# A hybrid block on one core: the plain slab of the second product stored in two parts, and the state space's outer products moved to GpSimd

## The chip, the cores and the metric

One core of a Trainium2 chip runs the whole block. The metric is device microseconds of one execution; lower is better.

## The reference, cut to what matters

`x` is 1024 positions by 1024 channels, all float32. `u`, `val`, `cg`, `bg`, `gs`, `gc` are column blocks of one input projection.

```python
xn = rmsnorm(x);  proj = xn @ w_in + b_in
y  = s5_branch(u)            # 32 groups of 16 channels, 64 complex states each, a linear scan over the positions
ya = (gelu(y) @ w_glu_a) * sigmoid(gelu(y) @ w_glu_b)
yb = (bg * conv3(cg * val)) @ w_conv_out
h  = x + (sigmoid(gs) * ya + sigmoid(gc) * yb) @ w_out
h  = h + square(relu(rmsnorm(h) @ w_ff1)) @ w_ff2      # 1024 -> 4096 -> 1024
return rmsnorm(h)
```

## The kernel before, in words

Activations lie transposed, channels on the 128 partitions and positions along the free dimension. A float32 operand is cut into a rounded high part and the rest, its low part (a Copy on ScalarE, a subtraction on VectorE), and one product of a 128x128 block is three matmuls of 512 columns: high by high, high by low, low by high. Every engine runs its instructions in the order in which the program issues them; no scheduler reorders them. Tiles come from rings of slots: `apool` (34 slots of 128x1024, tag "u"), `wpool` (6), `tpool` (6 slots of 128x512, `half`).

**The state space beside the projections.** `order` (line 146) lists 57 jobs on TensorE. The state space runs beside them as generators: `ssm_step(s)`, s = 0 to 7, two state groups each. `products` (line 131) adds to a credit account `BESIDE[job]` times 0.648 for each product and calls `draw` after every fourth; `draw` resumes the generators as long as the account is over zero, and each `yield` of a positive number is taken from it. A `yield` of a negative number lets the generator rest for so much of the planner's PE time. So the numbers in the `yield`s decide behind which product each piece of a step stands in every engine's order. A step computes two outer products (`outer`, line 473: a table `Bk` and a table `Vk`, each from two multiplications and two half-height subtractions or additions for the real and for the imaginary part), then phases on VectorE (`f`, `k`, `a1`), two Sin on ScalarE, four transposes of `Bk` (`pst`, line 523) and eight small matmuls of `Vk` by `Bk` (`psk`, line 526) on TensorE, a copy `WT` on ScalarE, the input matmuls (`psxr`, `psxi`, line 539), the scan on VectorE and the output matmuls (`psy`). Step s + 1 is started when the input matmuls of step s are issued. Before step 0, `ssm_params` computes the tables `dsc`, `asc`, `bbr`, `bbi`, `th`, `tl` on GpSimd.

**The feed-forward layer.** Its first product is done in 14 groups (`seven`, line 1204) of seven chains of 12 matmuls (P1 to P7 of a fast two-by-two scheme), with the callbacks `after(0)` to `after(6)` between them: P1, `after(0)`, P4 of the group before, `after(1)`, P5, `after(2)`, P2, `after(3)`, P6, `after(4)`, P3, `after(5)`, P7, `after(6)`. P4 adds into the bank `seed`, which `done(g, "c22")` reads on VectorE after P7 (line 1283). The last group has no group behind it, so its P4 follows its P7 at once. Results go to memory through GpSimd's DMA queue: groups 2 to 13 in the arrangement that the second product wants (the sums `t1` and `n2` already cut in a high and a low part, `split_out`, line 1256; the low part is made at the next `after`), groups 0 and 1 and the four plain blocks as whole rows `h2d`. The second product starts with a plain slab: the rows 24 to 27, which groups 0 and 1 wrote. `slab_load` (line 1160) fetches them at `after(0)` of the last group, and `slab_cut` (line 1166) cuts each into high and low in `after(3)` to `after(6)` of that group; `w2_cut(24)` fetches and cuts the first weight at `after(4)`. Then come 16 plain products (`pf`, line 1350), 12 groups of seven chains with the weights prepared by the lists `SECOND` (line 1075), and the last slab.

Of the kernel before, what the change touches and what calls it, by code (L numbers as in the profile page):

```python
# [9 lines left out]
F32 = mybir.dt.float32  # L10
F32R = mybir.dt.float32r
I32 = mybir.dt.int32
AF = mybir.ActivationFunctionType
ALU = mybir.AluOpType

P = 128
D = 1024
S = 1024
# [6 lines left out]
DFF = 4096  # L25
N_PLAIN = 4
N_GROUP = (32 - N_PLAIN) // 2
FIRST_PLAIN = 32 - N_PLAIN
N_CHUNK = 3
# [17 lines left out]
def block_kernel(ctx, tc, x_t, par, ssm, w_u, win, wco, wglu, wo, w1, w2, out):  # L47
    nc = tc.nc
    V, A, G, T = nc.vector, nc.scalar, nc.gpsimd, nc.tensor
# [8 lines left out]
    def unit(name, dt=F32):  # L58
        return apool.tile([P, S], dt, tag="u", name=name)

    def half(name, dt=F32):
        return tpool.tile([P, HALF], dt, tag="t", name=name)
# [4 lines left out]
    HS = [slice(0, HALF), slice(HALF, S)]  # L67
# [79 lines left out]
    for i in range(8):  # L147
        order.append(("val", i))
        if i in conv_out_after:
            r = conv_out_after[i]  # L150
# [26 lines left out]
    for k in range(8):  # L177
# [8 lines left out]
        t = unit(f"xr{k}")  # L186
# [272 lines left out]
    def sh(name):  # L459
        return swork.tile([P, HALF], F32, tag="sh", name=name)  # L460
# [4 lines left out]
    def ssm_step(s):  # L465

        q = slice(2 * s, 2 * s + 2)
# [5 lines left out]
        def outer(n, ar_, ai_, xr_, xi_, dst, first):  # L473
            w = 2 * n * 16
            ba = lambda z: z[:, q, :].unsqueeze(3).to_broadcast([P, 2, n, 16])
            bx = lambda z: z[:, q, :].unsqueeze(2).to_broadcast([P, 2, n, 16])
            for r in range(2):
                t = sh(f"o{s}_{n}_{r}")
                t1, t2 = (t[:, i * w:(i + 1) * w].rearrange("p (a l c) -> p a l c", a=2, l=n) for i in range(2))
                V.tensor_mul(t1, ba(ar_), bx(xi_ if r else xr_))  # L480
                V.tensor_mul(t2, ba(ai_), bx(xr_ if r else xi_))
                f = V.tensor_add if first == r else V.tensor_sub
                for g in range(2):
                    rows = slice(64 * g, 64 * g + 64)
                    f(dst[rows, :, r, :, g, :], t1[rows], t2[rows])

        outer(4, dsc_r, dsc_i, bbr, bbi, Bk.rearrange("p a r (j g c) -> p a r j g c", j=4, g=2), 1)
        yield 1.7
        outer(5, asc_r, asc_i, bc_raw[:, 2], bc_raw[:, 3], Vk.rearrange("p a r (l g c) -> p a r l g c", l=5, g=2), 0)
        yield 1.9  # L490


        th, tl = names["th"], names["tl"]
        f, k, a1 = sh(f"f{s}"), sh(f"k{s}"), sh(f"a{s}")
# [48 lines left out]
        xr, xi, t = sh(f"xr{s}"), sh(f"xi{s}"), sh(f"t{s}")  # L543
# [15 lines left out]
        yr, t2 = sh(f"yr{s}"), sh(f"t2{s}")  # L559
# [25 lines left out]
        if s % 2:  # L585
            for c in HS:
                y = U[s // 2].rearrange("p q c -> p (q c)")[:, c]
                t = sh(f"gz{s}_{c.start}")
# [65 lines left out]
    for k in range(8):  # L654
# [10 lines left out]
        for h in range(2):  # L665
            for e in range(3):
                wc = slice(o + e * P, o + (e + 1) * P)
                c = HS[h]
# [40 lines left out]
    h = [None] * 8  # L709
    wo_w = []  # L710
    dram = ctx.enter_context(tc.tile_pool(name="dram", bufs=1, space=bass.MemoryType.DRAM))
    hd = [dram.tile([P, S], F32, tag=f"hd{i}", name=f"hd{i}") for i in range(8)]
    h2d = {i: dram.tile([P, S], F32, tag=f"h2d{i}", name=f"h2d{i}") for i in range(8 * N_CHUNK, DFF // P)}
    xd = {
        (q, nm, part): dram.tile([P, 4, HALF], F32, tag=f"xd{q}{nm}{part}", name=f"xd{q}{nm}{part}")
        for q in range(N_CHUNK) for nm in X_OF.values() for part in ("hl" if nm in SPLIT else "r")
# [41 lines left out]
    for n in range(n_main):  # L758
        job = order[n]
        k, i = job[0], job[1]  # L760
# [49 lines left out]
        elif k == "val":  # L810
            cur["v"] = []
            for hh in range(2):
                t, t2 = half(f"v1_{n}_{hh}"), half(f"v2_{n}_{hh}")
# [3 lines left out]
        elif k == "cg":  # L817
            vp = spool.tile([P, S + 2], F32, tag="vp", name=f"vp{i}")
            V.memset(vp[:, 0:2], 0.0)
            for hh in range(2):  # L820
                t = half(f"c1_{n}_{hh}")
# [18 lines left out]
        elif k == "bg":  # L840
            vh, vl = unit(f"vh{i}", F32R), unit(f"vl{i}", F32R)
            for hh in range(2):
                t = half(f"b1_{n}_{hh}")
                t2 = half(f"b2_{n}_{hh}")
# [7 lines left out]
        elif k in ("gs", "gc"):  # L852
            if k == "gs":
                gs[i] = unit(f"gs{i}")
            for hh in range(2):
                t = half(f"g1_{n}_{hh}")
# [4 lines left out]
                else:  # L861
                    t2 = half(f"g2_{n}_{hh}")
                    A.activation(t2, t, AF.Sigmoid, bias=b)
                    V.tensor_mul(Y[i][:, HS[hh]], Y[i][:, HS[hh]], t2)
        elif k == "glu":
            mh, ml = unit(f"mh{i}", F32R), unit(f"ml{i}", F32R)
            for hh in range(2):
                pb, pa = ps[2 * hh], ps[2 * hh + 1]
                t, t2 = half(f"s1_{n}_{hh}"), half(f"s2_{n}_{hh}")
# [138 lines left out]
    def rows_of(g):  # L1008

        if g < 2:  # L1010
            return 8 * N_CHUNK + 2 * g, 8 * N_CHUNK + 2 * g + 1
        q, c = divmod(g - 2, 4)
        return 8 * q + c, 8 * q + 4 + c
# [53 lines left out]
    def steps_of(g, plan):  # L1067

        for step in plan:
            for what in step.split():  # L1070
                gw[g]["do"]["shl".index(what[0])](what[1])
            yield

    FIRST = ["", "", "s1 h0", "l0 h1", "l1"], ["s2 h2", "l2", "h3", "l3"]
    SECOND = ["", "", "", "s1 h3", "h1 l3", "l1"], ["s2 h0", "l0 h2", "l2"]

    def group_steps(g, own):

# [2 lines left out]
        if "do" not in gw[g]:  # L1081
            gw[g]["do"] = w_parts(g)
        return steps_of(g, (SECOND if g >= N_GROUP else FIRST)[own])

# [71 lines left out]
    slab = {}  # L1156
    raw2 = {}
    w2p = {}

    def slab_load(s):  # L1160
        for c in range(4):
            t = unit(f"fl{s}_{c}", F32R)
            nc.sync.dma_start(t.bitcast(F32), h2d[4 * s + c])
            raw2[s, c] = t

    def slab_cut(s, c):
        hi, lo = unit(f"fh{s}_{c}", F32R), raw2.pop((s, c))
        A.activation(hi, lo.bitcast(F32), AF.Copy)
        V.tensor_sub(lo, lo.bitcast(F32), hi.bitcast(F32))
        slab.setdefault(s, []).append((hi, lo))  # L1170
# [70 lines left out]
    def done(g, quad, ps, less):  # L1241

        i, hh = int(quad[1]) - 1, int(quad[2]) - 1
        if g >= N_GROUP:
            y = h[2 * ((g - N_GROUP) % 4) + i][:, HS[hh]]
            V.tensor_add(y, ps, y)
            if less is not None:
                V.tensor_sub(y, y, less)
            return
        paired = g >= 2  # L1250
        q, c = divmod(g - 2, 4)

        def out_of(name, t, part="r"):
            nc.gpsimd.dma_start(xd[q, name, part][:, c, :], t)

        def split_out(name, t, lo=None):

            hi = half(f"h{name}_{g}", F32R)
            A.activation(hi, t, AF.Copy)
            out_of(name, hi.bitcast(F32), "h")  # L1260

            def rest():
                V.tensor_sub((t if lo is None else lo).bitcast(F32R), t, hi.bitcast(F32))
                out_of(name, t if lo is None else lo, "l")
            waiting.append(rest)

        hold = held.setdefault(g, {})
        if paired and quad == "c11":
            hold.update({k: unit(f"hold{k}_{g}") for k in "a"})
        elif paired and quad == "c12":  # L1270
            hold.update({k: unit(f"hold{k}_{g}") for k in "b"})
        elif paired and quad == "c22":
            hold.update({k: unit(f"hold{k}_{g}") for k in "c"})
        if paired and quad != "c21":
            t = hold[{"c11": "a", "c12": "a", "c22": "c"}[quad]][:, HS[1 if quad == "c12" else 0]]
        else:
            t = half(f"{quad}_{g}")
        if less is None:
            r = half(f"r{quad}_{g}")
            A.activation(r, ps, AF.Relu)  # L1280
            V.tensor_mul(t, r, r)
        else:
            V.tensor_sub(t, ps, less)  # L1283
            relu_square(t)
        if not paired:
            nc.gpsimd.dma_start(h2d[rows_of(g)[i]][:, HS[hh]], t)
            return
        if quad != "c12":
            out_of(f"B{quad[1:]}", t)
        if quad == "c12":  # L1290
            t1 = hold["b"][:, HS[0]]
            V.tensor_sub(t1, hold["a"][:, HS[0]], t)
            split_out("t1", t1)
        elif quad == "c22":
            t3, n2 = hold["b"][:, HS[1]], hold["c"][:, HS[1]]
            V.tensor_sub(t3, hold["a"][:, HS[1]], t)
            V.tensor_sub(n2, hold["a"][:, HS[0]], t3)
            out_of("t3", t3)
            split_out("n2", n2, half(f"ln2_{g}"))
        elif quad == "c21":  # L1300
            t4 = half(f"t4_{g}")
            V.tensor_sub(t4, t, hold["c"][:, HS[1]])
            out_of("t4", t4)

    waiting = []

    plain_slab = 2 * N_CHUNK

    for g in range(N_GROUP):
        last_g = g == N_GROUP - 1  # L1310
        preps = [group_steps(g, 1), group_steps(g + 1, 0) if not last_g else iter(())]

        def after(i):
            for prep in preps:
                next(prep, None)
            while waiting:
                waiting.pop(0)()
            if i == 6 and g + 2 < N_GROUP:
                group_load(g + 2)
            if last_g:  # L1320
                if i == 0:
                    slab_load(plain_slab)
                elif 3 <= i:
                    slab_cut(plain_slab, i - 3)
                if i == 4:
                    w2_cut(4 * plain_slab)

        seven(g, after)
    last_product(N_GROUP - 1)
    while waiting:  # L1330
        waiting.pop(0)()


    h = []
# [6 lines left out]
    for j in range(16):  # L1341
        n, ii, hh = 4 * plain_slab + j // 4, (j // 2) % 2, j % 2
# [21 lines left out]
    for g in range(g0, g0 + 4 * N_CHUNK):  # L1364
        q, e = divmod(g - g0, 4)
# [69 lines left out]
    for c0 in range(0, S, LAST):  # L1435
        c = slice(c0, c0 + LAST)
# [3 lines left out]
        for e in range(8):  # L1440
            p = bank(f"pl{c0}_{e}")[:, :LAST]
            products(p, fw[e // 2], range(4 * (e % 2), 4 * (e % 2) + 4), xs, c)
            t = hf[e // 4][:, e % 4, :]
# [10 lines left out]
        for e in (6, 7):  # L1454
            t = hf[1][:, e - 4, :]
# [59 lines left out]
```

## Time and profile before

| | |
|---|---|
| time before, median of 3 runs | 1470.45 us (1469.85 to 1472.77) |
| profiled execution, its own time | 1471.11 us |
| span of that execution | 1469.3 us |
| mean granted clock of TensorE | 0.995 |
| TensorE busy | 1442.7 us of the span |
| VectorE, ScalarE, GpSimd busy | 998.4, 557.0, 150.4 us |

The span is from the first to the last instruction; 1.8 us of the execution's time lie outside it. PE is TensorE's matmuls, PEld its weight loads, DVE VectorE, ACT ScalarE, POOL GpSimd, SP the engine that issues most DMAs. A clock of 1.00 is 2.4 GHz, 0.50 is 1.2 GHz.

### The profile page before, as it was taken

Reading aid. Unit: us, or ns where it says so; the run is one execution under the profiler, and the core shown is the slowest. Engines: PE = TensorE matmul, PEld = TensorE weight load, DVE = VectorE, ACT = ScalarE, POOL = GpSimd, SP = SyncE. Lnnn points to the kernel's source line nnn. Section 1 sums busy time; section 2 is a strip of 40 time slices with the busy share of each in tenths; the row PEclk is TensorE's granted clock in tenths of the full one; section 3 lists DMA queues with packets and bytes.
Section 4 is the critical chain, followed back from the end, with each engine's and each line's share of the span. In section 5 each row is a group of like instructions: output and inputs, shape, how many; then the busy total and the mean of one; then the engine's idle time right before and its main releaser. Section 6 shows DMA issues by size and latency. Waiting matters only on the chain.

```text
span 1469.3 us, 17037 instructions
## 1 busy us (share of the span) xinstructions
PE 1442.7 (98%) x6563; PEld 1195.8 (81%) x6563; DVE 998.4 (68%) x1569; ACT 557.0 (38%) x804; POOL 150.4 (10%) x338
## 2 busy tenths in 40 slices
PE   9989999999999999999999999999998999999997
PEld 7868888888888888888888888888887878787897
DVE  7678487777878677447626875777776266758575
ACT  6541423223132236423313443333443443424254
POOL 5840000000000000000000011222222010000000
PEclk9999999999999999999999999999999999999999
DMA  5111111111111011115311243455558468445302
GB/s 217 29 43 44 43 43 44 43 43 58 31 56 44 30 43 43 58 44 186 128 45 58 86 133 121 179 177 177 178 190 294 156 173 261 169 152 220 116 28 88
DMA packets 47745, 156.90 MB, mean 107 GB/s; under 512 B 6064, under 2 KB 10544, under 8 KB 47664
## 3 DMA queue, kind: packets, MB, share of 16 engines
q1 hardware_dynamic: 35312, 114.92, 23.2%
q0 software_dynamic: 12352, 40.90, 8.1%
q8 instruction: 51, 0.84, 0.2%
q14 instruction: 30, 0.25, 0.1%
HBM read 114.90 MB, written 40.89 MB: 106 GB/s over the span
## 4 chain that ended last, share of the span: by engine, by line
PE 88%; DVE 6%; ACT 4%; issue 1%; DMA 1%; SPq 0%; DVEq 0%; ACTq 0%
PE ps L135 8%; PE ps L137 8%; PE ps L136 8%; PE seed L1089 5%; PE seed L1091 5%; PE seed L1090 5%; PE pa L1091 3%; PE pa L1089 3%; PE pa L1090 3%; PE pe L1091 3%; PE pe L1089 3%; PE pe L1090 3%; PE pc L135 2%; PE pg L137 2%; PE pc L136 2%; PE pg L135 2%
## 5 line engine op out<-in xcount | busy, mean ns | idle before, releaser
L135 PE MATMUL ps<-xh,wh 128*128 128x512 f32 x656 | 260.1, 396 | 1.2 <-ACT wh L95 1.1
L137 PE MATMUL ps<-xh,wl 128*128 128x512 f32 x656 | 256.1, 390 | 1.7 <-DVE wl L96 1.6
L136 PE MATMUL ps<-xl,wh 128*128 128x512 f32 x656 | 255.5, 389 | 0.0
L137 PEld LDWEIGHTS ps<-xh,wl 128*128 128x128 f32 x656 | 123.3, 188 | 29.5 <-DVE wl L96 3.6
L135 PEld LDWEIGHTS ps<-xh,wh 128*128 128x128 f32 x656 | 123.3, 188 | 28.7 <-ACT wh L95 2.4
L136 PEld LDWEIGHTS ps<-xl,wh 128*128 128x128 f32 x656 | 123.3, 188 | 25.3
L96 DVE TENSOR_TENSOR wl<-wr,wh 128x1024 fp32r<-128x1024 f32 x57 | 69.7, 1223 | 59.2 <-ACT wh L95 59.2
L894 POOL DMA_DIRECT2D hd<-h x16 | 8.9, 558 | 709.3 <-ACT ssum L896 634.1
L95 ACT ACTIVATE wh<-wr 128x1024 fp32r<-128x1024 f32 x57 | 59.6, 1047 | 52.3 <-PE pc L136 21.0
L1057 ACT ACTIVATE gh<-gs 128x1024 fp32r<-128x1024 f32 x52 | 55.0, 1058 | 33.4 <-DVE gs L1053 23.4
L1061 DVE TENSOR_TENSOR gl<-gs,gh 128x1024 fp32r<-128x1024 f32 x52 | 63.3, 1218 | 3.6 <-ACT gh L1057 3.6
L1061 DVE TENSOR_TENSOR gl<-rg,gh 128x1024 fp32r<-128x1024 f32 (+1 forms) x52 | 48.4, 950 | 5.4 <-ACT gh L1057 5.4
L135 PE MATMUL pc<-vh,wh 128*128 128x512 f32 x128 | 49.9, 390 | 0.0
L135 PE MATMUL pw<-mh,hwo 128*128 128x512 f32 x128 | 49.9, 390 | 0.0
L137 PE MATMUL pc<-vh,wl 128*128 128x512 f32 x128 | 49.8, 389 | 0.0
L137 PE MATMUL pw<-mh,lwo 128*128 128x512 f32 x128 | 49.8, 389 | 0.0
L136 PE MATMUL pw<-ml,hwo 128*128 128x512 f32 x128 | 49.8, 389 | 0.0
L137 PE MATMUL pg<-zh,wl 128*128 128x512 f32 x128 | 49.8, 389 | 0.0
L136 PE MATMUL pg<-zl,wh 128*128 128x512 f32 x128 | 49.8, 389 | 0.0
L135 PE MATMUL pg<-zh,wh 128*128 128x512 f32 x128 | 49.8, 389 | 0.0
L136 PE MATMUL pc<-vl,wh 128*128 128x512 f32 x128 | 49.8, 389 | 0.0
L1089 PE MATMUL seed<-xht,gh 128*128 128x512 f32 x112 | 44.7, 399 | 4.2 <-DVE holdc L1283 4.2
(528 smaller groups left out, 3540.7 us busy)
## 6 DMA issues: line engine op xcount, KB each, us to landing
rg<-in_w SPq DMA_DIRECT2D x52, 512.0 KB, 3.9
wr<-in_win SPq DMA_DIRECT2D x41, 512.0 KB, 3.6
wr<-in_wco SPq DMA_DIRECT2D x8, 512.0 KB, 3.5
wr<-in_wglu SPq DMA_DIRECT2D x8, 512.0 KB, 3.6
rwo<-in_wo SPq DMA_DIRECT2D x8, 512.0 KB, 6.7
h<-in_x_t SPq DMA_DIRECT2D x8, 512.0 KB, 7.4
hd<-h POOLq DMA_DIRECT2D x16, 256.0 KB, 2.3
fl<-h2d SPq DMA_DIRECT2D x8, 512.0 KB, 4.5
```

What stands on the lines that cost most here:

```text
L95: A.activation(hi, r, AF.Copy)
L96: V.tensor_sub(lo, r, hi.bitcast(F32))
L135: T.matmul(ps, wh[:, j, :], xh[:, cols], start=start and i == 0, stop=False)
L136: T.matmul(ps, wh[:, j, :], xl[:, cols], start=False, stop=False)
L137: T.matmul(ps, wl[:, j, :], xh[:, cols], start=False, stop=stop and i == n - 1)
L894: nc.gpsimd.dma_start(hd[i][:, c], h[i][:, c])
L1057: A.activation(hi[nm], src[nm], AF.Copy)
L1061: V.tensor_sub(lo[nm], src[nm], hi[nm].bitcast(F32))
L1089: T.matmul(p, wh[:, kb, :], xh, start=first and kb == 0, stop=False, skip_group_check=True)
L1090: T.matmul(p, wh[:, kb, :], xl, start=False, stop=False, skip_group_check=True)
L1091: T.matmul(p, wl[:, kb, :], xh, start=False, stop=kb == 3, skip_group_check=True)
```

## The change

Four edits. (1) All 16 instructions of a step's two outer products go from VectorE to GpSimd, and their two `yield`s, 1.7 and 1.9, become one of 0.1. (2) Groups 0 and 1 store their four results each through `split_out`: a high part made on ScalarE and a low part on VectorE, each with a DMA of its own, into new tensors `h2p`; at `after(2)` of the last group eight loads fetch both parts, and the four cuts of that slab go. (3) Low parts wait in `later` for one more `after` before they are made (`step_on`), in the paired groups too. (4) In `SECOND`, the high part "3" of the next group's weights is made at `after(2)` instead of `after(3)`, its low part with the sums at `after(3)`.

```diff
-                V.tensor_mul(t1, ba(ar_), bx(xi_ if r else xr_))
-                V.tensor_mul(t2, ba(ai_), bx(xr_ if r else xi_))
-                f = V.tensor_add if first == r else V.tensor_sub
+                G.tensor_tensor(t1, ba(ar_), bx(xi_ if r else xr_), op=ALU.mult)
+                G.tensor_tensor(t2, ba(ai_), bx(xr_ if r else xi_), op=ALU.mult)
                 for g in range(2):
                     rows = slice(64 * g, 64 * g + 64)
-                    f(dst[rows, :, r, :, g, :], t1[rows], t2[rows])
+                    G.tensor_tensor(
+                        dst[rows, :, r, :, g, :], t1[rows], t2[rows], op=ALU.add if first == r else ALU.subtract
+                    )
         outer(4, dsc_r, dsc_i, bbr, bbi, Bk..., 1)
-        yield 1.7
         outer(5, asc_r, asc_i, bc_raw[:, 2], bc_raw[:, 3], Vk..., 0)
-        yield 1.9
+        yield 0.1
...
-    SECOND = ["", "", "", "s1 h3", "h1 l3", "l1"], ["s2 h0", "l0 h2", "l2"]
+    SECOND = ["", "", "h3", "s1 l3", "h1", "l1"], ["s2 h0", "l0 h2", "l2"]
...
+    def slab_load_parts(s):
+        for c in range(4):
+            ts = []
+            for part in "hl":
+                t = unit(f"f{part}{s}_{c}", F32R)
+                nc.sync.dma_start(t.bitcast(F32), h2p[4 * s + c, part])
+                ts.append(t)
+            slab.setdefault(s, []).append(ts)
...
-        def split_out(name, t, lo=None):
-            hi = half(f"h{name}_{g}", F32R)
+        def split_out(dst, t, lo=None):
+            hi = half(f"h{quad}_{g}_{len(later)}", F32R)
             A.activation(hi, t, AF.Copy)
-            out_of(name, hi.bitcast(F32), "h")
+            nc.gpsimd.dma_start(dst("h"), hi.bitcast(F32))
             def rest():
                 V.tensor_sub((t if lo is None else lo).bitcast(F32R), t, hi.bitcast(F32))
-                out_of(name, t if lo is None else lo, "l")
-            waiting.append(rest)
+                nc.gpsimd.dma_start(dst("l"), t if lo is None else lo)
+            later.append(rest)
...
         if not paired:
-            nc.gpsimd.dma_start(h2d[rows_of(g)[i]][:, HS[hh]], t)
+            split_out(lambda part: h2p[rows_of(g)[i], part][:, HS[hh]], t)
             return
...
+    def step_on():
+        for f in waiting:
+            f()
+        waiting[:] = later
+        later.clear()
...
-            while waiting:
-                waiting.pop(0)()
+            step_on()
             if last_g:
-                if i == 0:
-                    slab_load(plain_slab)
-                elif 3 <= i:
-                    slab_cut(plain_slab, i - 3)
+                if i == 2:
+                    slab_load_parts(plain_slab)
                 if i == 4:
                     w2_cut(4 * plain_slab)
```

## Rows read from the trace of the kernel before

**Rows 1.** The waits of TensorE: us in total, times, longest us.

```profile
PE seed L1089 <- DVE holdc L1283: 4.2, 1, 4.2
...
PE psxr L539 <- ACT WT L529: 2.1, 1, 2.1
...
PE ps L137 <- DVE wl L96: 1.6, 3, 0.5
```

**Rows 2.** Stretches: length, PE, PEld, DVE, ACT, POOL busy, PEclk, DMA share, GB/s.

```profile
108.31:114.00 5.69, 5.69 (x18) 4.62 (x19) 2.32 (x3) 3.27 (x7) 0.00 (x0) 0.70 0.00 0
...
880.00:885.00 5.00, 5.00 (x24) 4.14 (x23) 2.74 (x5) 3.61 (x5) 0.41 (x1) 1.00 0.47 157
...
1110.00:1115.00 5.00, 5.00 (x24) 4.13 (x23) 3.47 (x4) 2.48 (x4) 1.10 (x3) 1.00 0.99 332
1123.63:1130.00 6.37, 6.37 (x16) 5.02 (x17) 4.13 (x6) 2.36 (x4) 2.17 (x4) 0.55 1.01 349
```

**Rows 3.** TensorE's timeline at step 0: start us, us, instruction, [idle before].

```profile
97.53 0.39 PE L137 MATMUL ps<-xh,wl 128*128 128x512 f32 x1
97.76 0.60 PE L523 MATMUL pst<-ident,Bk 128*128 128x128 f32 x4
98.29 1.06 PE L526 MATMUL psk<-Vk,Bk 128*32 128x128 f32 x8
...
108.31 0.76 PE L539 MATMUL psxr<-U,WT 128*128 128x256 f32 x2 [2.09 <-ACT WT L529]
...
111.07 0.99 PE L135 MATMUL ps<-xh,wh 128*128 128x512 f32 x1
```

**Rows 4.** VectorE's stretches in step 0: length, DVE busy (neighbours counted), PEclk, DMA share, GB/s.

```profile
89.79:94.77 4.98, 4.66 (x18) 1.00 0.36 105
94.77:96.49 1.72, 1.65 (x4) 1.00 0.00 0
103.53:107.03 3.50, 3.36 (x9) 1.00 0.51 150
```

**Rows 5.** GpSimd's timeline in the parameters of the state space.

```profile
43.97 0.25 POOL L291 TENSOR_TENSOR scratch<-scratch 128x32 f32<-128x32 f32 x1
...
81.48 0.62 POOL L294 TENSOR_TENSOR bbr<-bc_raw,scratch 128x256 f32<-128x256 f32 x1
...
82.76 1.07 POOL L300 TENSOR_TENSOR bbr<-bbr,bbt 128x256 f32<-128x256 f32 x1
...
87.94 0.25 POOL L444 TENSOR_SCALAR scratch<-scratch 128x16 f32<-128x16 f32 x1
...
93.65 0.22 POOL L297 TENSOR_TENSOR sp_tl<-sp_tl,scratch 128x16 f32<-128x16 f32 x1
```

**Rows 6.** TensorE's timeline behind the state space and at the products' ends.

```profile
579.73 0.50 PE L137 MATMUL ps<-xh,wl 128*128 128x512 f32 x1 [0.53 <-DVE wl L96]
...
1119.07 0.39 PE L1091 MATMUL seed<-xht,gl 128*128 128x512 f32 x1
1123.63 0.79 PE L1089 MATMUL seed<-xht,gh 128*128 128x512 f32 x1 [4.17 <-DVE holdc L1283]
...
1405.79 0.50 PE L1089 MATMUL seed<-xh2t,gh 128*128 128x512 f32 x1 [0.78 <-DVE ha L1246]
```

**Rows 7.** ScalarE's and VectorE's timelines in the last group of the first product.

```profile
1115.50 1.05 ACT L736 ACTIVATE hw<-rw 128x1024 fp32r<-128x1024 f32 x1
...
1116.78 1.22 DVE L737 TENSOR_TENSOR lw<-rw,hw 128x1024 fp32r<-128x1024 f32 x1
...
1121.75 1.23 DVE L1169 TENSOR_TENSOR fl<-fl,fh 128x1024 fp32r<-128x1024 f32 x1 [0.25 <-ACT fh L1168]
1122.89 0.68 DVE L1283 TENSOR_TENSOR holdc<-seed,sv 128x512 f32<-128x512 f32 x1
```

**Rows 8.** SP's issues: the last load of the slab, the next weight.

```profile
1101.59 0.32 SPq L1163 DMA_DIRECT2D fl<-h2d  x1
1102.01 0.38 SPq L731 DMA_DIRECT2D rw<-in_w  x1
```

More of the change, by code (lines that the diff above doesn't have):

```diff
@@ L712, in block_kernel @@
     hd = [dram.tile([P, S], F32, tag=f"hd{i}", name=f"hd{i}") for i in range(8)]
-    h2d = {i: dram.tile([P, S], F32, tag=f"h2d{i}", name=f"h2d{i}") for i in range(8 * N_CHUNK, DFF // P)}
+    h2d = {i: dram.tile([P, S], F32, tag=f"h2d{i}", name=f"h2d{i}") for i in range(FIRST_PLAIN, DFF // P)}
+    h2p = {
+        (i, part): dram.tile([P, S], F32, tag=f"h2{part}{i}", name=f"h2{part}{i}")
+        for i in range(8 * N_CHUNK, FIRST_PLAIN) for part in "hl"
+    }
     xd = {
@@ L1292, in done @@
             V.tensor_sub(t1, hold["a"][:, HS[0]], t)
-            split_out("t1", t1)
+            split_out(lambda part: xd[q, "t1", part][:, c, :], t1)
         elif quad == "c22":
@@ L1298, in done @@
             out_of("t3", t3)
-            split_out("n2", n2, half(f"ln2_{g}"))
+            split_out(lambda part: xd[q, "n2", part][:, c, :], n2, half(f"ln2_{g}"))
         elif quad == "c21":
@@ L1303, in done @@
             out_of("t4", t4)
-    waiting = []
+    waiting, later = [], []
+    def step_on():
[3 more added lines that the diff above has]
+        later.clear()
     plain_slab = 2 * N_CHUNK
@@ L1329, in block_kernel @@
     last_product(N_GROUP - 1)
-    while waiting:
-        waiting.pop(0)()
+    step_on()
+    step_on()
     h = []
```

## The prediction

> **What bounds the kernel now.** I read the waits of TensorE first. The table ahead has it busy for 1442.7 of 1469.3 us, so a change can win only where it idles or runs at the low clock, and it loses wherever it makes TensorE wait anew. Of the waits in the middle of the kernel the two longest are the two places that this change touches: 4.2 us on `holdc` at the end of the first product and 2.1 us on `WT` in the first step of the state space [rows 1]. The three waits on `wl`, 1.6 us together, are small. Next I read the granted clock in stretches behind both waits, since a wait can cost twice. From 108.31 to 114.00 it is 0.70 on the mean, a loss of 5.69 x 0.30 = 1.7 us; from 1123.63 to 1130.00 it is 0.55, a loss of 6.37 x 0.45 = 2.9 us [rows 2]. So the first place costs 2.1 + 1.7 and the second 4.2 + 2.9 us. At the end of the second product TensorE idles 0.78 us at the same kind of step, and the profile gives no low clock there [rows 6]. Then I read the timelines of each engine around both places, to see which instruction ends last.
>
> **The end of the first product.** P7 of the last group issues its last matmul at 1119.07, and P4 follows at 1123.63, as soon as VectorE has read `seed` (`holdc`) [rows 6, 7]. The reader is to see what stands in front of that read on VectorE: a slab cut of 1.23 us from 1121.75 [rows 7], and before it, by the program's order, the low part of `t1`, `lw` and two more slab cuts, each behind its high part on ScalarE. The change takes all four slab cuts away and moves the low part of `t1` behind the read. What is left is `lw`, 1.22 us, and the three operations of c12, each like the 0.68 us of `holdc`. ScalarE cuts the weight one slab cut earlier, about the 1.05 us of its own cut, so at 1114.5 instead of 1115.50 [rows 7]; VectorE then has `lw` done at about 1116.8 and c12 at about 1119.0, before P7 ends. So the read starts when P7 ends, as at 1405.79, where the idle time is 0.78 us [rows 6]. The wait shrinks by 4.17 - 0.78 = 3.4 us, and with it I count the 2.9 us of low clock as gone: **-6.3 us**. Bounds: nothing, if another wait takes its place (below), to 4.2 + 2.9 = -7.1 us.
>
> **What the two parts cost elsewhere.** Groups 0 and 1 make eight more high parts on ScalarE, eight more low parts on VectorE and eight more DMAs on GpSimd's queue. In a stretch of group 1 VectorE is busy 2.74 of 5.00 us, ScalarE 3.61, GpSimd 0.41, the DMA share is 0.47 and TensorE has no gap [rows 2], so idle time of those engines takes them in: I cost them at nothing. Without that cover each low part would be a half of a 1.22 us cut, eight of them 4.9 us [rows 7]. The low parts that come a step later feed only DMAs to tensors that are read much later. They hold two `half` slots longer, and the ring has six; in the paired groups each high part stays until its low part is made, one step of 2.7 us (12 matmuls of 0.23 [rows 3]) longer. I cost that at nothing too. The list `SECOND` puts the high part "3" one chain earlier and removes nothing: nothing.
>
> **The outer products, steps 1 to 7.** Sixteen instructions in 4.98 us leave VectorE in each step [rows 4]. TensorE does not wait for VectorE there except 0.53 us at 579.73 [rows 6], behind the work that the planner drains at the end; with smaller `yield`s the steps finish earlier, so I count **-0.5 us** (0 to -0.5). GpSimd is idle there and may start as soon as `Bk` is free, long before the transposes of that step.
>
> **The outer products, step 0.** Here the change is on the path. First the planner's account, worked through from the code. At the first `draw` of the `bg` job at place 3 of `order` it stands at 1.41; each `draw` of that job earns 0.38 x 2.59 = 0.98, of the next, `val`, 0.62 x 2.59 = 1.61. Before: 1.41 - 1.7, + 0.98 - 1.9, + 0.98, + 0.98 - 1.7, then in `val` + 1.61 - 2.3, + 1.61, + 1.61 - 1.2, and the transposes come at the third `draw` of `val`, behind its 12th product. After: 1.41 - 0.1 - 1.7, + 0.98 - 2.3, + 0.98, + 0.98 - 1.2, and the transposes come at `val`'s first `draw`, behind its 4th product. A product is three matmuls of 0.23 (97.53 to 97.76 [rows 3]), 0.68 us, so TensorE meets the transposes 8 x 0.68 = 5.4 us earlier: at 92.3 instead of 97.76.
>
> On GpSimd the outer products stand behind all parameters, whose last instruction ends at 93.65 + 0.22 = 93.9 [rows 5]; on VectorE they had begun at 89.79 [rows 4]. No row shows this operation on GpSimd. Its own time I take between a two-input operation of 32 columns, 0.25 us, and one of 256, 0.62 us [rows 5], in proportion: 0.41 us for 128 columns, 0.46 for 160, so 8 x 0.41 + 8 x 0.46 = 7.0 us for the 16. With VectorE at work beside it the seven large operations from 81.48 to 87.94 took 6.46 us, 0.92 each, 1.49 times the 0.62 [rows 5]; each held-up one took 1.07. I take 1.49, since VectorE is again busy without a gap (its own pieces of this step, 1.72 and 3.50 us [rows 4], now stand there): 10.4 us, so GpSimd ends at 104.3. Bounds: 7.0 us (100.9) and 16 x 1.07 = 17.1 us (111.0).
>
> TensorE stands behind the transposes from 92.3, but for 0.6 us of them, and behind `psk` until 104.3; with `psk`, 1.06 us [rows 3], it goes on at 105.3. To the point behind the input matmuls and the 12 products of `val` and 4 of `cg` that preceded them before, it has 16 products, 10.9 us, and the input matmuls, half of the 111.07 - 108.31 = 2.76 us that they took at the low clock [rows 3], 1.4 us: 117.6. After so long a wait I count the dearer of the two low clocks, 2.9 us [rows 2]: 120.5. Before, the same point was reached at 111.07, with 0.3 us of low clock to come: 111.4. So **+9.1 us**; the old wait on `WT` is gone within it, because that copy is now made while TensorE stands. Behind the waiting transposes stand only TensorE's own next products. VectorE waits too: `f` needs `th`, so it begins about 93.5, and behind it the read of the finished `bg` banks comes some 5 us later than now; TensorE, still standing, needs none of it before 105. Bounds: +4.4 (7.0 us on GpSimd, 1.7 us of clock) and +15.8 (17.1 us).
>
> A rule that speaks against this edit: the Trainium skill, page "SBUF — State Buffer", section "Who interferes with whom", says that a VectorE instruction with two SBUF inputs and a GpSimd instruction that reads SBUF block each other for a whole instruction. By that rule VectorE's work of this step would stand between GpSimd's instructions as in the second rival, and the time would be that rival's. The rows agree in part: the 0.62 and the 1.07 us are the same shape with and without a neighbour.
>
> **The sum.** +9.1 - 6.3 - 0.5 = +2.3 us on the profiled execution's 1471.1 us, which is 0.7 above the median shown: 1470.45 + 2.3 = **1472.8 us**. About 0.2%, 2.9 us, is what a measurement of this kernel tells from no change.
>
> **The rivals.** All times as medians.
> - *Forecast, 0.54.* Own range from the cheap end (+4.4 - 6.8 = -2.4: 1468.0) to GpSimd's 7.0 us plus VectorE's 5.2 us of this step between them (106.1, +10.9 - 6.8 = +4.1: 1474.5). Of its chance 0.38 lies within 0.2%, 0.16 above.
> - *Lockstep, 0.15.* VectorE and GpSimd alternate for all 16 instructions: 5.2 us are 11 VectorE instructions [rows 4], 16 of them 7.6 us, so GpSimd ends at 93.9 + 7.0 + 7.6 = 108.5, +13.3 - 6.8 = +6.5: 1476.9. For it: the 1.07 us rows. Against it: the mean of the seven is 0.92, and VectorE waits for other engines in between once its own pieces are through.
> - *The slab's eight loads delay the weight, 0.13.* Eight loads of 0.5 MB in place of four, all ahead of the weight in SP's queue, in a stretch whose DMA share is 0.99 already [rows 2]. Before, the last of the four went out at 1101.59 and the weight at 1102.01 [rows 8]; now four more stand in front, 2.1 MB, 6 us at 332 GB/s. Their slots come free with the holds of group 11 and with the operand of P1, so five of the eight go out within a few us. It decides once the weight lands later than about 1115; the loads behind it on SP feed the second product, some 20 us later. At 2 us more the read of `seed` is late again (idle 3 us, the low clock back): -1.2 instead of -6.3, sum +7.4: 1477.9.
> - *Faster, 0.14.* GpSimd's own price (100.9), and the clock is up again before TensorE has work, as the wait falls into the low stretch: +2.7 - 6.8 = -4.1: 1466.4. It decides below about 0.45 us for an instruction. For it: the 0.22 to 0.25 us of small operations at 93.65 with VectorE busy [rows 5].
> - *The account comes out as before, 0.04.* The transposes stay at 97.76 and wait there for GpSimd until 104.3; some 6.0 - 2.6 + 1.2 = +4.6 - 6.8 = -2.2: 1468.3, no change.
>
> Faster 0.14, within 0.2% 0.38 + 0.04 = 0.42, slower 0.16 + 0.15 + 0.13 = 0.44. The range, 1467.5 to 1478.0, leaves out the faster case and the upper ends of the second and third, 0.2 together.
>
> **What the profile after would show.** Right: a wait of TensorE at `pst` and `psk` on GpSimd between 92 and 105 and a low clock behind it; no wait on `WT`; `seed` waiting some 0.8 us for `holdc`, the clock 1.00 there; 16 GpSimd instructions from 94 in about 10 us. Wrong, if the transposes find `Bk` ready, if the wait at the end of the first product keeps its size or its clock, or if a new wait stands in groups 0 to 2 on a `half` slot.

## The result

The changed kernel takes 1478.72 us (median of 4 runs, 1478.36 to 1480.26) against 1470.15 us (4 runs, 1469.83 to 1472.77) for the kernel before on the same chip: a ratio of 1.0056, 95% interval [1.0039, 1.0074]. That is slower by more than the 0.2% that the prediction set as the least difference to be told from none, 5.9 us above the predicted time and 0.7 us beyond the upper end of its range. The profiled execution takes 1478.85 us, span 1477.1, granted clock 0.990.

TensorE's waits in the profile after (us in total, times, longest):

```profile
PE pst L523 <- POOL Bk L484: 5.6, 2, 3.5
PE psk L526 <- POOL Vk L484: 4.2, 2, 2.3
PE pa L1095 <- DVE gl L1065: 3.4, 3, 2.1
PE seed L1093 <- DVE holdc L1297: 3.3, 1, 3.3
```

Against [rows 1], the wait on `WT` is gone and two waits on GpSimd stand in its place, 9.8 us together; the wait on `holdc` is only 0.9 us shorter. TensorE's timeline around the first, and at the end of the first product:

```profile
92.85 0.39 PE L137 MATMUL ps<-xh,wl 128*128 128x512 f32 x1
96.73 0.47 PE L523 MATMUL pst<-ident,Bk 128*128 128x128 f32 x1 [3.49 <-POOL Bk L484]
99.26 0.90 PE L523 MATMUL pst<-ident,Bk 128*128 128x128 f32 x3 [2.06 <-POOL Bk L484]
102.15 0.64 PE L526 MATMUL psk<-Vk,Bk 128*32 128x128 f32 x2 [1.99 <-POOL Vk L484]
105.05 1.49 PE L526 MATMUL psk<-Vk,Bk 128*32 128x128 f32 x6 [2.26 <-POOL Vk L484]
106.47 0.80 PE L135 MATMUL ps<-xh,wh 128*128 128x512 f32 x1
...
1130.41 0.79 PE L1093 MATMUL seed<-xht,gh 128*128 128x512 f32 x1 [3.26 <-DVE holdc L1297]
```

GpSimd's timeline, some outer products of step 0 (VectorE busy beside them) and of step 1 (`L480` and `L481` are the multiplications, `L484` the half-height additions and subtractions):

```profile
93.80 0.22 POOL L297 TENSOR_TENSOR sp_tl<-sp_tl,scratch 128x16 f32<-128x16 f32 x1
93.98 0.64 POOL L480 TENSOR_TENSOR o<-dsc_r,bbr 128x128 f32<-128x128 f32 x1
...
102.18 0.79 POOL L480 TENSOR_TENSOR o<-asc_r,bc_raw 128x160 f32<-128x160 f32 x1
102.93 0.45 POOL L481 TENSOR_TENSOR o<-asc_i,bc_raw 128x160 f32<-128x160 f32 x1
103.46 1.54 POOL L484 TENSOR_TENSOR Vk<-o 64x160 f32<-64x160 f32 x2
...
112.31 0.46 POOL L480 TENSOR_TENSOR o<-asc_r,bc_raw 128x160 f32<-128x160 f32 x1
112.73 0.46 POOL L481 TENSOR_TENSOR o<-asc_i,bc_raw 128x160 f32<-128x160 f32 x1
```

VectorE beside the two multiplications of 102.18 and 102.93 (in step 1, from 109.42 to 114.00, it is idle):

```profile
101.84 0.81 DVE L854 TENSOR_TENSOR vl<-b,vh 128x512 fp32r<-128x512 f32 x1 [0.70 <-ACT vh L853]
102.57 0.68 DVE L849 TENSOR_TENSOR b<-ps,rstd 128x512 f32<-128x512 f32 x1
```

GpSimd takes from 93.98 to 105.00, 11.0 us, for step 0, and TensorE goes on within 0.1 us of each of its four ends. SP's issues and the cut of the weight that stands behind them:

```profile
1109.27 0.32 SPq L1170 DMA_DIRECT2D fl<-h2l  x1
...
1111.85 1.16 SPq L1170 DMA_DIRECT2D fl<-h2l  x1
1113.11 1.25 SPq L735 DMA_DIRECT2D rw<-in_w  x2
...
1125.38 1.06 ACT L740 ACTIVATE hw<-rw 128x1024 fp32r<-128x1024 f32 x1 [3.03 <-DMA rw<-in_w]
...
1126.47 1.23 DVE L741 TENSOR_TENSOR lw<-rw,hw 128x1024 fp32r<-128x1024 f32 x1 [4.89 <-ACT hw L740]
...
1129.67 0.68 DVE L1297 TENSOR_TENSOR holdc<-seed,sv 128x512 f32<-128x512 f32 x1
```

Five of the eight slab loads go out between 1109.27 and 1113.0, the weight behind them, and it lands 12.2 us after its issue. ScalarE waits 3.03 us for it, VectorE stands 4.89 us in front of `lw`, and c12 and the read of `seed` come after that. Stretches of the same profile (length, busy times, PEclk, DMA share, GB/s):

```profile
95.76:109.42 13.66, 6.38 (x19) 4.16 (x20) 9.41 (x14) 5.12 (x10) 12.58 (x21) 0.50 0.10 27
...
1115.00:1125.00 10.00, 10.00 (x46) 8.29 (x45) 3.25 (x5) 2.32 (x4) 1.63 (x3) 1.00 1.03 408
...
1130.41:1136.78 6.37, 6.37 (x22) 5.18 (x23) 3.85 (x6) 2.18 (x4) 2.92 (x6) 0.76 0.98 325
1187.43:1192.43 5.00, 5.00 (x15) 3.97 (x16) 3.64 (x4) 2.79 (x4) 0.00 (x0) 0.66 0.59 203
```

While the weight is under way the DMA engines are full. Behind the wait on `seed` the clock is 0.76 on the mean, not 1.00 as forecast; and it is low once more behind a wait of 2.11 us at the start of the second product. The kernel before has the same wait of 2.11 us, and the clock of its next 5.00 us is 1.00:

```profile
PE pa L1091 <- DVE gl L1061: 3.4, 3, 2.1
...
1181.96 0.50 PE L1091 MATMUL pa<-xh0B,gl 128*128 128x512 f32 x1 [2.11 <-DVE gl L1061]
...
1181.96:1186.96 5.00, 5.00 (x22) 4.13 (x23) 3.63 (x4) 2.81 (x4) 0.00 (x0) 1.00 0.56 203
```

The first of these lines stands between the two that [rows 1] shows. So the prediction's sentence that the two longest waits in the middle are the two places of the change is not right: this one, which the change leaves as it is, is as long as the wait on `WT` (2.09 us).

**Where the 7.8 us of the span come from.** The same TensorE instruction in both traces, after less before: at the wait on `wh` that ends at 77.36 before, 0.9 us (nothing is changed ahead of it; in e3 and e2, below, it ends at 76.99 and 78.63); at the sums behind the state space (812.73 and 820.45) 7.7; at the end of the wait on `seed` (1123.63, 1130.41) 6.8; at the wait of 2.11 us (1181.96, 1187.43) 5.5; at the next group's wait (1259.51, 1266.57) 7.1; at the last wait (1462.45, 1469.38) 6.9; at the end of the span 7.8. So the state space loses 6.8 us; the end of the first product wins 0.9 us of wait and 1.3 us of clock; 1.6 us of clock are lost again in the second product; and 0.9 us each lie at the start and at the end, in code that is the same. Half of the last 0.9 us is clock: the last two matmuls take 1.22 us at 0.50, against 0.70 us before. The first 0.9 us are not quite a loss apart, since TensorE then waits for GpSimd, which began step 0 only 0.1 us later than its parameters had ended before (93.98 against 93.87).

### The profile page after: what moved, and what is told of

Read it like the earlier page. It is cut to its first block, busy times and chain, and to the rows that moved or that the text cites. A ratio compares the mean times of both kernels' runs of the same rounds, so it can differ in the third digit from the quotient of the medians.

```text
span 1477.1 us, 17137 instructions
## 1 busy us (share of the span) xinstructions
PE 1445.2 (98%) x6563; PEld 1198.2 (81%) x6563; DVE 967.4 (65%) x1445; ACT 552.1 (37%) x803; POOL 223.6 (15%) x474
## 4 chain that ended last, share of the span: by engine, by line
PE 88%; POOL 5%; DVE 3%; issue 1%; DMA 1%; ACT 1%; SPq 0%; DVEq 0%; ACTq 0%; POOLq 0%
PE ps L135 9%; PE ps L137 9%; PE ps L136 9%; PE seed L1093 5%; PE seed L1095 5%; PE seed L1094 5%; PE pa L1095 3%; PE pa L1094 3%; PE pa L1093 3%; PE pe L1093 3%; PE pe L1095 3%; PE pe L1094 3%; PE pc L135 2%; PE pc L137 2%; PE pg L136 2%; PE pg L135 2%
## 5 line engine op out<-in xcount | busy, mean ns | idle before, releaser
L861 DVE TENSOR_TENSOR g<-ps,rstd 128x512 f32<-128x512 f32 x32 | 21.7, 687 | 41.5 <-PE ps L137 41.4
```

Of the source, the lines that this page charges most:

```text
L861: V.tensor_mul(t, ps[hh], rstd[:, HS[hh]])
```

## Experiments

My theory: step 0 waits for GpSimd, and the slab's loads delay the weight. Each run has its own rival. Every ratio is to the kernel before, run beside it on the same chip.

**e1_slab_only**: the changed kernel with the state space of the kernel before.

```diff
-                G.tensor_tensor(t1, ba(ar_), bx(xi_ if r else xr_), op=ALU.mult)
-                G.tensor_tensor(t2, ba(ai_), bx(xr_ if r else xi_), op=ALU.mult)
+                V.tensor_mul(t1, ba(ar_), bx(xi_ if r else xr_))
+                V.tensor_mul(t2, ba(ai_), bx(xr_ if r else xi_))
+                f = V.tensor_add if first == r else V.tensor_sub
...
+                    f(dst[rows, :, r, :, g, :], t1[rows], t2[rows])
...
+        yield 1.7
...
-        yield 0.1
+        yield 1.9
```

> The slab's parts alone, with the state space's outer products left on VectorE. Theory (the eight loads of the slab stand ahead of the weight of the second product on SP's queue and make it land late): at the end of the first product TensorE still waits about 3.3 us for its seed, as in the changed kernel (3.26 us, against 4.17 us in the kernel before), with one stretch of 3.4 us at the lower clock behind it instead of 6.8 us, so 0.7 to 2.3 us are won and the time is 1468 to 1469.5 us. Rival (the loads do no harm, it is GpSimd's load in the changed kernel that delayed the end of the first product): the wait falls to about 0.8 us, no stretch at the lower clock follows, and the time is about 1464 us. In both the state space's stage is as in the kernel before.

Measured: 1470.76 us, 0.9995 [0.9986, 1.0005]. SP's issue of the weight, and its cut:

```profile
1104.70 1.21 SPq L735 DMA_DIRECT2D rw<-in_w  x2
...
1117.11 1.06 ACT L740 ACTIVATE hw<-rw 128x1024 fp32r<-128x1024 f32 x1 [2.97 <-DMA rw<-in_w]
```

The wait on `seed` is 3.20 us, so the slab's loads alone make it; the rival is out. The time lies above the forecast of 1468 to 1469.5 us: behind that wait the clock is 0.73, and 0.66 behind the 2.11 us wait; the forecast had counted the first alone.

**e2_outers_only**: the kernel before with the change to `outer` and its yield.

> The outer products on GpSimd alone, with the one short yield of the change, and the slab as before. Theory (all of the loss is in step 0 of the state space): TensorE waits for Bk and Vk of step 0 some 9.8 us in all between 93 and 105 us, a stretch of 13.7 us at the lower clock lies over it, and the time is 1476 to 1478 us, 6.8 us above the kernel before. Rival (the loss lies with the slab's parts, and the state space's is made good by what GpSimd takes off VectorE in the steps behind): at most 1472 us.

Measured: 1478.66 us, 1.0051 [1.0037, 1.0066], just above the forecast. The waits on `Bk` and `Vk` are 3.8 and 4.2 us, somewhat less than forecast (TensorE came 0.4 us later and GpSimd began 0.9 us earlier than in the changed kernel). With e1, the two halves add up within their intervals: +0.0051 - 0.0005 against +0.0056 for the whole.

**e3_gpsimd_old_yields** and **e4_vector_new_yield** take the two parts of that edit apart. e3 has the instructions of `outer` on GpSimd and the yields of the kernel before (1.7 between the two calls of `outer`, 1.9 behind them); e4 has them on VectorE and the one yield of the change:

```diff
-        yield 1.7
...
-        yield 1.9
+        yield 0.1
```

> The outer products on GpSimd, but with the two yields of the kernel before (1.7 and 1.9), so that step 0's transposes stay where they stood, behind the twelfth product of val. Theory (the loss is GpSimd's end at 105.0 us less the time at which TensorE comes to wait for it, and eight more products of 0.65 us stand ahead of the wait): some 5.2 us of the 6.8 us are given back, and the time is 1471 to 1474 us. Rival (GpSimd's slowness delays something else as well, such as VectorE's f of step 0, and the place does not matter): 1476 us or more.

Measured: 1476.27 us, 1.0034 [1.0021, 1.0046]; above what the theory gave and just within the rival's range. Its waits:

```profile
PE psk L527 <- POOL Vk L484: 5.2, 2, 3.1
...
PE pst L524 <- POOL Bk L484: 1.6, 1, 1.6
```

TensorE waits 6.8 us, not 4.6. In this execution it came to the wait on `wh` 1.3 us earlier than in the changed kernel (76.99 against 78.24), but GpSimd ended step 0 at 105.63, 0.6 us later: its 16 instructions took 12.05 us from 93.58 (the first pair for `Vk` 2.12 us, against 1.53; with the old yields it stands beside VectorE's long cut of a weight, `wl`, 1.23 us from 100.59). And the clock of the 6.00 us behind is 0.53, a loss of 2.8 us. So the place of the transposes gives back about 2.5 us of 7.5 (1.0051 to 1.0034, whose intervals overlap), not 5.2. The rival's delay of something else is not seen: up to 822 us these two waits are the only ones of TensorE that the kernel before does not have.

> The outer products left on VectorE, and only the yields changed as in the change (0.1 in all in place of 1.7 and 1.9), so that the transposes of each step are drawn eight products earlier. Theory (it is GpSimd's duration with the early place that costs, 11.0 us for sixteen instructions): VectorE ends Bk and Vk of step 0 near 95 us, TensorE waits 2 to 3 us there instead of 9.8 us, and the time is 1470 to 1473 us. Rival (the early place alone is the loss, whatever the engine): 1476 us or more.

Measured: 1477.73 us, 1.0038 [1.0023, 1.0053]. The theory is wrong here: the early place costs on VectorE too, by another wait. ScalarE's timeline, and TensorE's wait:

```profile
101.07 0.63 ACT L848 ACTIVATE vh<-b 128x512 fp32r<-128x512 f32 x1 [0.76 <-DVE b L845]
103.85 0.63 ACT L848 ACTIVATE vh<-b 128x512 fp32r<-128x512 f32 x1 [2.15 <-DVE b L845]
104.38 1.04 ACT L95 ACTIVATE wh<-wr 128x1024 fp32r<-128x1024 f32 x1
105.33 0.58 ACT L528 ACTIVATE WT<-pst 128x512 f32<-128x512 f32 x1
...
PE psxr L538 <- ACT WT L528: 5.3, 1, 5.3
```

Drawn at one go, step 0 fills VectorE from 89.17 to 99.6; both `b` of `v` come behind it, both `vh` wait for `b`, and the copy `WT` stands behind them on ScalarE, while TensorE has come to the input matmuls eight products earlier. It waits 5.3 us instead of 2.1, and two more waits stand at 258 and 359 us, 1.0 and 1.2 us, which the kernel before does not have. So the new yields and the new engine each cost some 5 us alone, and 7.5 us together: they fill the same time, since `WT` is made while TensorE stands for GpSimd.

**e5_weight_first**: the changed kernel, with the weight ahead of the slab's loads.

```diff
+                if i == 0:
+                    held["w2"] = raw_load(w2[4 * plain_slab], f"w2_{4 * plain_slab}")
                 if i == 2:
                     slab_load_parts(plain_slab)
                 if i == 4:
-                    w2_cut(4 * plain_slab)
+                    w2p[4 * plain_slab] = cut(held.pop("w2"), f"w2_{4 * plain_slab}", wtile)
```

> The changed kernel with one edit: the weight of the second product's first plain strip is issued ahead of the slab's eight loads instead of behind them; its cut stays where it was. Theory (the weight lands 12 us after its issue behind the loads, and VectorE's cut of it holds up c12 and c22 behind it): ACT's cut no longer waits for the DMA, TensorE's wait for the seed falls from 3.26 to about 0.8 us, with or without the stretch of 3.4 us at the lower clock behind it, so 2.5 to 4.2 us are won on the changed kernel and the time is 1474.5 to 1476.2 us. Rival (the order of the loads does not matter, VectorE's own work sets the wait): the wait stays above 3 us and the time is that of the changed kernel, 1478.7 us.

Measured: 1474.77 us, 1.0025 [1.0016, 1.0034], as the theory said. SP's issue of the weight, VectorE's cut and read, TensorE's wait, and the stretch behind it:

```profile
1098.06 0.33 SPq L735 DMA_DIRECT2D rw<-in_w  x1
1098.62 0.33 SPq L1170 DMA_DIRECT2D fh<-h2h  x1
...
1123.30 1.23 DVE L741 TENSOR_TENSOR lw<-rw,hw 128x1024 fp32r<-128x1024 f32 x1 [2.07 <-ACT hw L740]
...
1127.16 0.69 DVE L1297 TENSOR_TENSOR holdc<-seed,sv 128x512 f32<-128x512 f32 x1 [0.57 <-PE seed L1095]
...
1127.91 0.50 PE L1093 MATMUL seed<-xht,gh 128*128 128x512 f32 x1 [0.78 <-DVE holdc L1297]
...
1127.91:1134.28 6.37, 6.37 (x28) 5.25 (x29) 4.04 (x6) 2.74 (x4) 3.55 (x7) 1.00 1.01 347
```

Now the read of `seed` waits for TensorE's own P7, the wait is 0.78 us, and the clock behind it 1.00: the picture that the prediction had drawn for the change. ScalarE cuts the weight at 1122.21, 4.9 us before P7 ends at 1127.13; the prediction's 1114.5 meant 5.0.

**e6_step0_vector**: the changed kernel with step 0 back on VectorE with the old yields; **e7_both**: e6 with the edit of e5; **e8_slab_weight_first**: e1 with the edit of e5.

```diff
+            E = V if s == 0 else G
...
+        if s == 0:
+            yield 1.7
...
-        yield 0.1
+        yield 1.9 if s == 0 else 0.1
```

> The changed kernel with step 0's outer products and yields as in the kernel before (VectorE, 1.7 and 1.9), and steps 1 to 7 as in the change (GpSimd, 0.1). Theory (the whole loss lies in step 0, where GpSimd's parameters end only at 94 us): the 9.8 us of waits for Bk and Vk are gone, the wait of 0.5 us at 580 us is gone as in the changed kernel, and the time is 1468 to 1470 us. Rival (the short yields cost in the later steps too, as they do with the outer products on VectorE, where two waits of 1.0 and 1.2 us stood in steps 1 and 2): 1472 us or more.

> Both mends at once: step 0's outer products on VectorE with the old yields, and the weight ahead of the slab's loads. Theory (the two losses are independent): the sum of both, 1464 to 1467 us, faster than the kernel before. Rival (what is won at the end of the first product is lost again in the stretch at the lower clock that follows the next waits): 1468 us or more.

> The slab's parts with the weight ahead of their loads, and the state space entirely as before. Theory (the slab's half of the change gives its gain once the weight is in time): TensorE's wait for the seed falls from 4.17 to about 0.8 us, the time is 1464.5 to 1467.5 us, and about 1 us above the kernel with both mends, which also lacks the wait at 580 us. Rival (the slab's half gives nothing, whatever the order): about 1470 us.

Measured: e6 1468.89 us, 0.9984 [0.9974, 0.9994]; e7 1464.72 us, 0.9956 [0.9941, 0.9971]; e8 1467.01 us, 0.9964 [0.9950, 0.9978]. All three times came as the theory said. The weight's place is worth the same in three pairs: changed kernel to e5 0.0031, e1 to e8 0.0031, e6 to e7 0.0028, so 4.1 to 4.6 us, of which 2.3 to 2.5 us are the wait, 1.5 to 1.7 the clock behind it, and up to 0.6 are not accounted for. GpSimd in steps 1 to 7 is worth 0.0008 to 0.0011 (e7 with e8, e6 with e1); the intervals overlap, so these times alone do not show it, but the traces of e6 and e8, whose clock is 1.00 there, agree: from the wait on `WT` to the sums behind the state space TensorE takes 701.7 us (109.97 to 811.71) and 702.8 us (109.40 to 812.20).

**e9_order_only**: the kernel before with `step_on` and the new `SECOND` alone.

> The kernel before with only the two small parts of the change: the low parts a step later, and the second product's steps in the new order; the slab and the state space as before. Theory (these two cost and bring nothing, as the waits of the second product kept their sizes in the changed kernel): 1470 to 1472 us, no difference from the kernel before, with the waits of 0.8 and 2.1 us at the start of the second product unchanged. Rival (they take part in the loss): 1473 us or more.

Measured: 1471.61 us, 0.9998 [0.9988, 1.0009]; the waits at the second product's start are 0.81 and 2.11 us, as in the kernel before. These parts cost nothing.

**e10_b22_earlier**: e7, with the cut of B22 a step earlier.

```diff
-        if j % 3 == 0 and 0 < j < 15:
+        if j % 3 == 0 and 0 < j:
             x_cut(0, names_x[j // 3 - 1])
...
                         x_load(0, "t3")
-                        x_cut(0, "B22")
```

> The kernel with both mends, and one step of the second product moved: the cut of its operand B22 one step earlier, with the last product of the plain slab instead of behind the first product of its group. It stands there ahead of the group's own weights on ACT (2.0 us) and VectorE (2.4 us), and TensorE waits 0.8 and 2.1 us for these. Theory (these two waits are the cause of the lower clock that follows them in some executions): both waits fall by some 2 us together, no stretch at the lower clock is left between 1110 and 1440 us, and the time is 1461.5 to 1463.5 us. Rival (the cut earlier delays the seed's copy or the first product, and the waits come back under another name): 1464.5 us or more.

Measured: 1464.86 us, 0.9951 [0.9937, 0.9965], the time of e7: the rival. The two waits became one under another name, with the clock at 0.66 in the 5.00 us behind it:

```profile
PE pe L1098 <- DVE gl L1068: 2.0, 1, 2.0
```

The cut now stands on VectorE ahead of a low part of the group's weights that it had followed. Putting that low part first was not tried.

**e11_step0_split**: e7, with `Vk` of step 0 on GpSimd (`E = V if s == 0 and n == 4 else G`).

> The kernel with both mends, with half of step 0's outer products given back to GpSimd: Bk on VectorE, Vk on GpSimd, the yields of step 0 as in the kernel before. Theory (what counts is when GpSimd ends, not that it does the work: it starts at 94 us, eight instructions take some 5.5 us, and TensorE needs Vk only near 98.5 us): TensorE waits about 1 us for Vk, not 9.8 us, and the time is 1464 to 1466.5 us. Rival (any outer product of step 0 on GpSimd stalls TensorE as in the changed kernel): 1468 us or more.

Measured: 1463.82 us, 0.9946 [0.9929, 0.9963], the fastest of all, though its interval overlaps e7's. GpSimd begins at 93.36 and ends `Vk` at 99.42:

```profile
PE psxr L542 <- ACT WT L532: 1.6, 1, 1.6
PE psk L529 <- POOL Vk L485: 0.2, 1, 0.2
```

The same engine costs TensorE 0.2 us there, because TensorE needs `Vk` only at 99.2.

**The clock behind the two waits**, from the same view of each trace: the wait on `seed` with PEclk in the 6.37 us from its end, and the wait of 2.1 us at the start of the second product with PEclk in the 5.00 us from its end.

| kernel | wait on `seed` | PEclk | second wait | PEclk |
|---|---|---|---|---|
| before | 4.17 | 0.55 | 2.11 | 1.00 |
| e9 | 4.11 | 0.56 | 2.11 | 1.00 |
| e2 | 4.17 | 0.51 | 2.11 | 0.50 |
| e3 | 4.17 | 0.73 | 2.11 | 0.66 |
| e4 | 4.17 | 0.75 | 2.11 | 0.66 |
| changed | 3.26 | 0.76 | 2.11 | 0.66 |
| e1 | 3.20 | 0.73 | 2.11 | 0.66 |
| e6 | 3.13 | 0.73 | 2.11 | 0.50 |
| e5 | 0.78 | 1.00 | 2.11 | 0.66 |
| e8 | 0.78 | 1.00 | 2.11 | 0.50 |
| e10 | 0.79 | 1.00 | 1.99 (`pe`) | 0.66 |
| e7 | 0.78 | 1.00 | 2.11 | 1.00 |
| e11 | 0.78 | 1.00 | 2.12 | 1.00 |

The same wait of 4.2 us is followed by 0.51 to 0.75, the same wait of 2.11 us by 0.50 to 1.00. Only where the wait is 0.78 or 0.79 us is the clock the same in all executions. What decides between the levels at the longer waits stays open; one execution of each kernel was profiled.

## Why the prediction was wrong

**The step that failed is the end of the first product, -6.3 us.** Its sentence on the weight, that ScalarE cuts it "at 1114.5 instead of 1115.50", looked at the order on ScalarE and VectorE and took the weight to be there. It was not: in e1, where the state space is as in the kernel before, the cut comes at 1117.11, as soon as the weight has landed. The term measured -0.9 us of wait and -1.3 us of clock. The third rival, with 0.13, had the place, the cause and the point (later than about 1115, 2 us more, idle 3 us); it happened, with 3.26 us. What it under-rated is how surely it would come: the weight went out some 3 us later than before (1104.70 in e1 against 1102.01) and then took 12.4 us to land in a full stretch, against 7.3 in the kernel before (no run takes these two apart). A row that the prediction did not read would have told it: 1102.01 and 7.3 us to landing, with the 6 us that the rival itself counts, make 1115.3, already past its own point of 1115. e5 and e8 show that the term was right in all but the order on SP's queue: with the weight first, the wait is 0.78 us, as said, and e8 gains 5.3 us (0.9964) for the 6.3.

**The 2.9 us of clock within it** were not firmly the wait's. The one execution that they were read from had 0.55 behind the wait; others with the same wait had 0.51 to 0.75. The changed kernel lost 1.5 us there and 1.7 us behind a wait in the second product, which the prediction had no reason to price, since the same wait stood in the kernel before at 1.00.

**Step 0, +9.1 us.** The mechanism came step by step as said: TensorE at the transposes at 93.2 (92.3 said, and the whole execution is 0.9 us later there), GpSimd through at 105.0 (104.3), no wait on `WT`. The prediction's price of an instruction, between the free and the held-up rows, was close: 11.0 us for 16 against 10.4. The point that it put at 120.5 us was reached at 120.62, and behind it TensorE is 8.8 us later than in the kernel before. That it comes out so exactly is luck: the clock was over-sized (TensorE takes up its products at 106.47 and the low clock ends near 109.4, 1.5 us of loss for the 2.9 counted), while GpSimd ended 0.7 us later than said and `psk` ran at the low clock. Steps 1 to 7 gave about 1.0 us for 0.5. With them the stage measured 7.7 us in this trace, 6.8 when its late start is taken off, and 7.5 in e2, against 9.1 - 0.5 = 8.6.

**Lockstep** did not happen: it had GpSimd end at 108.5, and it ended at 105.0. The prediction let every VectorE instruction of the step stand in GpSimd's way; the rows show that it depends on which. The four multiplications of 128x160 in step 0 took 0.79, 0.45, 0.79 and 0.45 us: the long ones began beside `f<-f,k` and `vl<-b,vh`, whose two inputs lie in SBUF, the short ones beside `b<-ps,rstd`, one of whose inputs lies in PSUM, and 0.46 us is their time in step 1 with VectorE idle. [rows 5] has the same: VectorE was at work beside the 0.62 us too, with a multiplication that reads `ps`, so "with and without a neighbour" is not what these rows show. The rule named with it, of the Trainium skill's page "SBUF — State Buffer", section "Who interferes with whom", speaks of VectorE instructions with two SBUF inputs; these rows agree with it, and the time of the second rival does not follow from it.

**What was costed at nothing** cost nothing: there is no new wait between 106 and 1126 us, and e9 gives 0.9998.

So the sum, +2.3, missed because 6.3 us of gain were 0.6 us when the clock in the second product is counted in. The state space came 0.9 us cheaper than its 8.6, with the late start in it, and the 0.9 us at the end of this execution took that back.

## What to carry to other kernels

When a change puts more loads into a queue, first find what stands behind them in it, work out when that lands, and see who needs it first: here one weight behind eight loads undid most of the slab's gain of about 5 us, and moving its issue ahead gave it back. A slower engine is priced by when it ends against when its result is needed, not by its own time: the same outer products cost 5 us, with the new yields 7.5, where TensorE stood waiting for them, gave back about 1 us in the seven other steps, and made a wait of 0.2 us when half of the first step's were left there. And a planner's due times are part of an edit: changed alone, with no other engine, they cost 5.6 us, by a wait two engines further on.

## What the runs showed of the hardware

Three things I had not expected. The clock behind one and the same wait differs between executions of kernels that have the same code there (the table above), so a loss of 2 to 3 us at a low clock, read from one profile, is one draw rather than a price. And a load of 0.5 MB issued behind five others of its size took 12.2 us to land, in a stretch of 408 GB/s and a DMA share of 1.03. The five ahead of it took 4.9, 5.8, 8.2, 9.8 and 11.9 us, in the order of their issue; the same weight, issued first in e5, took 4.2 us. Place in the queue was what counted. And whether VectorE holds up a GpSimd instruction depended on VectorE's inputs: 0.79 us beside two in SBUF, 0.45 us beside one in PSUM, for the same multiplication of 128x160.
